# Block 0's W_O by seven products, the next operands from W_B on, and one scores matmul for two pairs

## The chip, the cores and the metric

The kernel runs on one core of a Trainium2 chip. The metric is the device time of one execution in microseconds, taken as the median of several runs. The profile names the engines PE (TensorE, matrix products), PEld (its weight loads), DVE (VectorE), ACT (ScalarE), POOL (GpSimd) and SP (SyncE, which here only issues DMA).

## The reference

One layer is computed for 2048 prompt tokens and 64 sample tokens, all in float32, model width 1024.

```
h = rms_norm(x, g_pre);  vA, bA, cA, zA, q, f, iv, zB, gA, gB = split(h @ w_in)     # ten 1024-wide parts
yA = (silu(zA) * bA * causal_conv3(cA * vA, conv_w)) @ w_a_out                      # path A
fg = lb + (1 - lb) * sigmoid(f);  k = 1 - fg;  qq = silu(q) * QK_SCALE              # path B, 8 heads of 128
per chunk of 64 tokens:
    att = tril(qe @ ke^T);  o = att @ v + (q * exp(b)) @ S;  S = exp(b_last) * S + (k * ...)^T @ v
yB = (rms(o) * g_onorm * silu(zB)) @ w_b_out
merged = sigmoid(gA) * yA + sigmoid(gB) * yB
x = x + rms_norm(merged @ w_o, g_post)
x = x + (p @ w_ple_proj) * sigmoid(rms_norm(x, g_ple) @ w_ple_gate)
```

The outputs are the new x of both streams and the end states of the convolution and of S.

## The kernel before

The 2112 tokens stand on the free axis, features on the 128 partitions. They are cut into three blocks of 704 columns, numbered 0, 1 and 2, and every block into two halves of 352 (`HN`). Each float32 operand is split into a rounded high part and the rest (`split`: a ScalarE copy and a VectorE subtraction), and each product is three matmuls: high by high, high by low, low by high. The weights are split likewise. In block 0 the low halves are made on VectorE and stored to DRAM under a key in `lows`; later uses load them (`split_w`). The stores go to SP's queue in block 0 and to POOL's queue from block 1 on.

Most of the large products save an eighth of their matmuls by taking seven products of quarter matrices instead of eight (Strassen's scheme in Winograd's form). In `sgroup` the seven run side by side for one pair of weight blocks. In `in_turn` they run one after the other over four groups each: a product's seven operands are made in turn by VectorE and ScalarE (`operand_of`) while the product before it runs, so that the operands of the whole stage need not be held. Both need four sums S1 to S4 of weight quarters, which stand in DRAM under `sums`; `combined` makes them in block 0 for the parts of w_in, `prepare_sums` for W_A, W_B and W_O (`w_a_out`, `w_b_out`, `w_o`), four groups for each matrix.

A block goes through these stages: eight heads of path B (`head_prep`, then `head_attn` in steps) mixed with gate products; path A (`path_a`); W_A; W_B with the merge by the gates; W_O; then the first gates of the next block, into which the norm of this block (`final_norm`) is spread, and the gate product W_G with the end of the layer (`final_gate`). In block 0, W_A, W_B and W_O are plain: `gemms` runs eight output blocks of 2 halves x 8 feature blocks x 3 matmuls, that is 48. In blocks 1 and 2 all three go by `in_turn`. The sums of W_A and W_B are prepared during W_A and W_B of block 0 (`sums_ahead`, from `merge`), those of W_O during path A of block 1.

While W_O runs, the operands of the next block's gates are made (`operands`: two x tiles are loaded and scaled, then eight combinations of their halves are formed and split; four such quarters). In block 0 this goes with W_O's output blocks 1, 3, 5 and 7, in block 1 through hooks. Hooks are small steps queued in `hooks`; one is taken after each product or group, so that their instructions stand in the queues right there. In block 0 the squares for the norm are summed as W_O's outputs come (`final_out`); in block 1 they are summed in the first hooks of the next gates (`squares`).

In a head, a pair is two chunks of 64 tokens. A block has five pairs and a lone chunk; four pairs stand in part 0, the fifth in part 1, the lone chunk in part 2. `head_prep` makes kb (a pair's keys, the first chunk scaled to the second) and ka (the first chunks' keys, unscaled). `head_attn` transposes kb and v on TensorE (L935, L937), then makes the scores: for each pair one matmul of ka by the first chunk's queries (L946, 64 columns) and one of kb by the second chunk's (L947). L946 takes 128 columns of ka, which hold the first chunks of two neighbouring pairs, and only one pair's half of the result is used. The mask `caus` and `copy_predicated` (L950, L951) put the scores into `att`. `sink_v` writes v by `into` (L412), one VectorE instruction for each half.

The order of the instructions on each engine is that of the program, moved by a scheduler that weighs priorities (`tc.high_priority`) and marks (`placed`, `behind_all`). Large tiles come from a ring of 52; PSUM has five banks for products (`pg`) and three for the rest (`pa`).

Of the kernel before, what the change touches and what calls it, by code (L numbers as in the profile page):

```python
# [90 lines left out]
def hybrid_step(  # L91
# [61 lines left out]
    caus = const.tile([P, P], I32, tag="caus", name="caus")  # L153
# [14 lines left out]
    def constants():  # L168
        tri = rt(P)
        G.memset(tri, 1.0)  # L170
        G.affine_select(
            out=tri, in_=tri, pattern=[[1, P]], compare_op=ALU.is_ge, fill=0.0, base=0, channel_multiplier=-1
        )
        V.tensor_copy(caus, tri)
# [414 lines left out]
    def gemms(idx0, act, segs, by_k=False, late=KB - 1):  # L589

        j0, j1 = 0, KB
        if len(segs) > 1:
            yield from gemm_late([idx0, idx0 + 1], act, segs, late)
            j0 = 2
        if by_k:
            j1 -= 2
        for j in range(j0, j1):
            yield gemm(idx0 + j, act, segs)
        if by_k:
            yield from gemm_by_k([idx0 + j for j in range(j1, KB)], act, segs)  # L600
# [235 lines left out]

    def head_prep(bl, hc, hd, first, hs):
# [24 lines left out]
        ka, kb, qx, vt, z = hf(HN + 32), rt(), rt(), rt(), rt()  # L862

        def scaled(after):
# [8 lines left out]
            for g in bl["groups"]:  # L873
# [6 lines left out]
            V.tensor_tensor(chunks(kb)[:, 1:nch:2, :], chunks(sf)[:, 1:nch:2, :], chunks(lg)[:, 1:nch:2, :], ALU.mult)  # L880
            V.tensor_tensor(
                chunks(kb)[:, 0 : 2 * npair : 2, :],
                ka3[:, :npair, :],
                f2.unsqueeze(2).to_broadcast([P, npair, CH]),
                ALU.mult,
            )
# [6 lines left out]
        def sink_v(c, h, x, y):  # L893
            if c == 1:
                into(half(vt, h), x, y)
# [13 lines left out]
    def head_attn(ip, gs, d, hd):  # L909
# [21 lines left out]

        p_k, p_v = ps_attn(), ps_attn()
# [9 lines left out]
        with placed():  # L942
            for i, g in enumerate(gs):
                o = g["off"]
                if not single:
                    T.matmul(p_a[:, i * P : i * P + CH], d["ka"][:, o // 2 : o // 2 + P], qe[:, o : o + CH], start=True, stop=True)  # L946
                T.matmul(p_a[:, i * P + CH : i * P + P], cols(d["kb"], g), qe[:, o + ln - CH : o + ln], start=True, stop=True)  # L947
        pa3 = cols3(p_a, nt)
        if not single:
            V.copy_predicated(att[:CH, :nt], caus[:CH].unsqueeze(1).to_broadcast([CH, nt, P]), pa3[:CH])  # L950
        V.copy_predicated(att[CH:, :nt, CH:], caus[CH:, CH:].unsqueeze(1).to_broadcast([CH, nt, CH]), pa3[CH:, :, CH:])  # L951
# [138 lines left out]
    def merge(bl, a, kept, extra):  # L1090

        segs = bl["segs"]
        ob, m, mg, loaded = [], [], [], {}
# [19 lines left out]
        for j, pss in enumerate(gemms(W_B, ob, segs)):  # L1113
# [8 lines left out]
        return mg  # L1122
# [34 lines left out]
    def final_out(segs, mg, xo, acc):  # L1157

        for j, pss in enumerate(gemms(W_O, mg, segs, True)):
            xo.append(rt())  # L1160
            for s, ps in zip(segs, pss):
                A.copy(xo[j][:, cols_of(s)], ps)
            if j < KB - 2:
                sum_squares(j, xo[j], acc, BN)
            yield
        for j in range(KB - 2, KB):
            sum_squares(j, xo[j], acc, BN)
        yield

# [20 lines left out]
    def final_norm(bl, segs, xo, acc, h2, kept, squares=False):  # L1190
# [15 lines left out]
        if squares:  # L1206
# [172 lines left out]
    for bi, bl in enumerate(blocks):  # L1379
# [10 lines left out]
        sums_ahead = prepare_sums((W_A, W_B), True) if first else prepare_sums((W_O,), False) if bi == 1 else iter(())  # L1390
# [17 lines left out]
        if first:  # L1408
            mg = merge(bl, a, kept, sums_ahead)
        else:  # L1410
            stages, loads = merge_in_turn(a, kept, mg)
            stages.append(out_in_turn(mg, xo, acc, bl["last"]))
            loads(W_A, -1)
            for idx, n in in_turn(stages, a_first):
                loads(idx, n)
                if nxt and (idx, n) == (W_B, 6):
                    hc = new_operands()
                    ops = operands(hc, spread_all(cols), partial(load_x, nxt), True)
                    spread_out((ops, (0, 1, 0, 1, 0, 1, 0) * KH))
                elif nxt:  # L1420
                    pass
                elif (idx, n) == (W_B, 5):
                    ph = [split_rt(raw) for raw in load_p(bl, G)]
                elif (idx, n) == (W_O, 4):
                    norms = [final_norm(bl, [s], xo, acc, h2, None) for s in segs]
                    spread_out((norms[0], (1, 0, 1, 1, 1, 0, 1, 0)))
            if nxt:
                xo.extend(stages[-1]["mid"])
        if nxt:
            if first:  # L1430
# [68 lines left out]
```

## Time and profile before

| | us |
|---|---|
| median of 3 runs | 2639.74 |
| lowest and highest | 2634.62, 2641.88 |
| the profiled execution | 2640.08 |
| its span | 2638.4 |
| TensorE busy in it | 2610.8 |
| VectorE, ScalarE, GpSimd busy | 1708.9, 1483.9, 360.0 |

The stages by the trace, in microseconds from the span's start: heads and path A of block 0 to 664.9, its W_A to 726.5, W_B to 788.2, W_O from 789.5 to 853.9, the first gates of block 1 to 956.5, W_G of block 0 to 1018.4. Block 1 has W_A from 1534.4, W_B from 1588.8, W_O from 1644.5 to 1702.1, then the gates of block 2 to 1807.4. A group's line in the profile reads: source line, engine, operation, written and read tiles, shape, count, then busy microseconds, mean nanoseconds of one, and the idle time before them with what ended it. A busy span of a matmul is longer than the step from one to the next, since they are pipelined; steps are read from start to start.

### The profile page before, as it was taken

The numbers are of one execution on the slowest core, as the hardware profiler recorded it, in microseconds if no ns is written. First come the engines' busy times: TensorE is split into PE (matmuls) and PEld (weight loads), VectorE is DVE, ScalarE is ACT, GpSimd is POOL, SyncE is SP. The second block draws the span as 40 slices with busy tenths as digits, with TensorE's granted clock in tenths as the row PEclk, the third lists the DMA queues.
The fourth block names the chain that finished last, engine by engine and source line by source line (L and its number), as shares of the span: only waits on it lengthen the run. The fifth ranks groups of instructions, "written<-read, shape, count | busy, mean of one in ns | idle before, by whom it ended". The sixth has DMA issues, their size and how long they took to land. (4 is left out here: it accounts for less than half of the span.)

```text
span 2638.4 us, 47798 instructions
## 1 busy us (share of the span) xinstructions
PE 2610.8 (99%) x16700; PEld 2593.0 (98%) x16700; DVE 1708.9 (65%) x3325; ACT 1483.9 (56%) x2892; POOL 360.0 (14%) x665
## 2 busy tenths in 40 slices
PE   8999999999999999999999999999999999999999
PEld 8999999999999999999999999999999999999998
DVE  7788888888666554665645569763356464337867
ACT  6666665554335644665645555664466564445664
POOL 1000000200432211111112211021000000001011
PEclk9999999999999999999999999999999999999999
DMA  8677777998998998767789989898767768888975
GB/s 308 225 269 274 246 279 263 313 312 283 377 339 288 346 307 276 222 198 265 224 286 360 378 309 329 282 357 310 255 222 226 232 221 263 272 271 311 310 243 186
DMA packets 364530, 741.29 MB, mean 281 GB/s; under 512 B 44448, under 2 KB 49088, under 8 KB 364288
## 3 DMA queue, kind: packets, MB, share of 16 engines
q1 hardware_dynamic: 326016, 590.30, 66.5%
q0 software_dynamic: 37984, 147.90, 15.4%
q8 instruction: 131, 2.15, 0.3%
q14 instruction: 111, 0.91, 0.1%
q10 hardware_dynamic: 288, 0.05, 0.0%
HBM read 532.00 MB, written 206.06 MB: 280 GB/s over the span
## 5 line engine op out<-in xcount | busy, mean ns | idle before, releaser
L366 PE MATMUL pg<-r,hi 128*128 128x352 f32 x3304 | 1095.3, 332 | 1.9 <-ACT hi L222 0.7
L367 PE MATMUL pg<-r,hi 128*128 128x352 f32 x3304 | 1068.0, 323 | 0.0
L368 PE MATMUL pg<-r,lo 128*128 128x352 f32 x2356 | 763.2, 324 | 2.8 <-DMA lo<-low 2.8
L222 ACT CAST hi<-raw 128x512 fp32r<-128x512 f32 x720 | 443.0, 620 | 569.8 <-PE pg L367 204.9
L366 PEld LDWEIGHTS pg<-r,hi 128*128 128x128 f32 x3304 | 622.8, 189 | 5.9 <-issue 3.7
L367 PEld LDWEIGHTS pg<-r,hi 128*128 128x128 f32 x3304 | 623.1, 189 | 0.0
L368 PEld LDWEIGHTS pg<-r,lo 128*128 128x128 f32 x2356 | 444.0, 188 | 3.5 <-DMA lo<-low 3.5
L368 PE MATMUL pg<-r,s 128*128 128x352 f32 x948 | 306.7, 323 | 0.8 <-DMA s<-low 0.8
L546 PE MATMUL pg<-r,hi 128*128 128x352 f32 x768 | 248.0, 324 | 0.5 <-ACT hi L192 0.5
L547 PE MATMUL pg<-r,hi 128*128 128x352 f32 x768 | 247.9, 323 | 0.3 <-DVE r L192 0.3
L192 ACT CAST hi<-raw 128x512 fp32r<-128x512 f32 x234 | 142.6, 619 | 160.3 <-PE pg L367 44.5
L548 PE MATMUL pg<-r,lo 128*128 128x352 f32 x688 | 222.5, 323 | 0.3 <-DVE lo L192 0.2
L512 PE MATMUL pg<-r,hi 128*128 128x352 f32 x656 | 212.4, 325 | 0.0
L511 PE MATMUL pg<-r,hi 128*128 128x352 f32 x656 | 209.4, 325 | 0.3 <-ACT r L192 0.2
L192 DVE TENSOR_TENSOR r<-r,r 128x352 fp32r<-128x352 f32 (+3 forms) x282 | 173.2, 633 | 54.6 <-ACT r L192 53.6
L192 DVE TENSOR_TENSOR lo<-raw,hi 128x512 fp32r<-128x512 f32 x234 | 159.2, 686 | 68.3 <-ACT hi L192 55.3
L192 ACT CAST r<-r 128x352 fp32r<-128x352 f32 (+3 forms) x282 | 153.2, 576 | 50.1 <-DVE r L692 15.1
L368 PEld LDWEIGHTS pg<-r,s 128*128 128x128 f32 x948 | 178.3, 188 | 1.2 <-DMA s<-low 1.1
L192 ACT CAST hi<-s 128x512 fp32r<-128x512 f32 x160 | 99.1, 619 | 141.9 <-PE pg L367 115.5
L380 ACT COPY hf<-pg 128x352 f32<-128x352 f32 x354 | 155.6, 447 | 5.1 <-PE pg L368 4.5
L546 PEld LDWEIGHTS pg<-r,hi 128*128 128x128 f32 x768 | 144.2, 188 | 1.2 <-ACT hi L192 0.8
L547 PEld LDWEIGHTS pg<-r,hi 128*128 128x128 f32 x768 | 144.3, 188 | 0.7 <-DVE r L192 0.6
(388 smaller groups left out, 4177.5 us busy)
## 6 DMA issues: line engine op xcount, KB each, us to landing
raw<-w_blk SPq DMA_DIRECT2D x586, 256.0 KB, 4.1
lo<-low SPq DMA_DIRECT2D x412, 256.0 KB, 4.0
raw<-S SPq DMA_DIRECT2D x408, 256.0 KB, 4.2
low<-lo SPq DMA_DIRECT2D x338, 256.0 KB, 3.8
s<-low SPq DMA_DIRECT2D x308, 256.0 KB, 3.9
S<-s SPq DMA_DIRECT2D x152, 256.0 KB, 3.3
r<-w_blk POOLq DMA_DIRECT2D x48, 256.0 KB, 7.3
S<-r POOLq DMA_DIRECT2D x48, 256.0 KB, 6.1
```

Of the source, the lines that this page charges most:

```text
L192: return A.copy(hi, src).ins, V.tensor_tensor(lo, src, hi.bitcast(F32), ALU.subtract).ins
L222: A.copy(hi, raw)
L366: add(hi[:, k, :], xhi, start=start and k == 0, stop=False)
L367: add(hi[:, k, :], xlo, start=False, stop=False)
L368: last[0] = add(lo[:, k, :], xhi, start=False, stop=k == KH - 1).ins
L380: copied = A.copy(got[n], ps[bank])
L511: add(hi[:, k, :], xhi, start=start and k == 0, stop=False)
L512: add(hi[:, k, :], xlo, start=False, stop=False)
L546: T.matmul(ps, hi[:, k % 4, :], xhi[:, c], start=k == ks[0], stop=False)
L547: T.matmul(ps, hi[:, k % 4, :], xlo[:, c], start=False, stop=False)
L548: last[0] = T.matmul(ps, lo[:, k % 4, :], xhi[:, c], start=False, stop=k == ks[-1]).ins
```

## The change

Block 0's W_O goes by `in_turn`, as in the other blocks, with `merge` handing over unsplit merged tiles. Its weight quarters have no stored low halves yet, so they are split and stored there. The sums of W_O and W_A are prepared in W_A and W_B of block 0, those of W_B in path A of block 1. The operands of the next block start earlier: one quarter in W_B (block 0 after output blocks 3, 5, 6 and 7, block 1 in hooks of products 5 and 6), the rest in hooks of W_O. The spread of the row norms by TensorE moves with them. The squares and the norm of block 0 follow the plan that block 1 has.

In the heads, the odd pairs hold their second chunk first. So one matmul of ka by the first chunks' queries of two pairs puts each pair's scores on the rows where that pair has its first chunk, and L946 becomes three matmuls a head instead of five, two of them 128 columns wide. For this kb is made by four instructions instead of two, v is written in eight pieces instead of two (`in_order`), and there is a second mask, so that the copies of part 0 go by even and odd pairs.

```
+        for rows, odd, base in ((slice(0, P), 0, 0), (slice(0, CH), 1, -CH), (slice(CH, P), 1, CH)):
...
-    def operands(hc, rs, load, early=False):
-        pair = None
+    def operands(hc, rs, load):
+        pair = [load(k) for k in (0, KH)]
+        yield
         for i in range(KH):
-            pair = pair or [load(k) for k in (i, i + KH)]
...
-            pair = [load(k) for k in (i + 1, i + 1 + KH)] if early and i + 1 < KH else None
+            pair = [load(k) for k in (i + 1, i + 1 + KH)] if i + 1 < KH else None
+    def in_order(nch, npair):
+        out = []
+        for c in range(nch):
+            g, second = divmod(c, 2)
+            to = CH * (c + (1 - 2 * second if g % 2 and g < npair else 0))
+            cut = HN if c * CH < HN < (c + 1) * CH else (c + 1) * CH
+            for lo, hi in ((c * CH, cut), (cut, (c + 1) * CH)):
...
+            for odd in range(2):
+                seconds = slice(1 + 2 * odd, 2 * npair, 4)
+                gs = slice(odd, npair, 2)
...
+                V.tensor_tensor(chunks(kb)[:, place[1], :], chunks(sf)[:, seconds, :], chunks(lg)[:, seconds, :], ALU.mult)
+                V.tensor_tensor(chunks(kb)[:, place[0], :], ka3[:, gs, :], scale, ALU.mult)
-                into(half(vt, h), x, y)
+                for o, end, to in pieces:
+                    if h * HN <= o < (h + 1) * HN:
+                        s = slice(o - h * HN, end - h * HN)
+                        V.tensor_tensor(vt[:, to : to + end - o], x[:, s], y[:, s], ALU.add)
-                if not single:
-                    T.matmul(p_a[:, i * P : i * P + CH], d["ka"][:, o // 2 : o // 2 + P], qe[:, o : o + CH], start=True, stop=True)
+                if not single and i % 2 == 0:
+                    both = slice(i, min(i + 2, nt))
+                    own = cols3(p_a, nt)[:, both, :CH]
+                    firsts = qe[:, o : o + (both.stop - i) * P].rearrange("p (g c) -> p g c", c=P)[:, :, :CH]
+                    T.matmul(own, d["ka"][:, o // 2 : o // 2 + P], firsts, start=True, stop=True)
-            mg.append(split_rt(sg))
+            mg.append(sg)
...
+            side(j)
-        sums_ahead = prepare_sums((W_A, W_B), True) if first else prepare_sums((W_O,), False) if bi == 1 else iter(())
+        sums_ahead = prepare_sums((W_O, W_A), True) if first else prepare_sums((W_B,), False) if bi == 1 else iter(())
+        stages = [out_in_turn(mg, xo, acc, bl["last"])]
+        if first:
+            def side_ops(j):
+                if j == KB - 2:
+                    a_first.extend(narrow(half(t, 0)) for t in mg[:KH])
+                if j in (3, 5, 6, 7):
+                    next_ops(1)
+            merge(bl, a, kept, mg, sums_ahead, side_ops)
...
+        rest = (0, 1, 0, 1, 0, 1, 0, 0, 0) * (KH - 1)
+        if first:
+            spread_out((ops, rest))
+        for idx, n in in_turn(stages, a_first):
+            loads(idx, n)
+            if nxt and (idx, n) == (W_B, 4):
+                next_ops(1)
+                spread_out((ops, (0, 0, 0, 1, 0, 1, 0, 1) + rest))
-                for j, _ in enumerate(final_out(segs, mg, xo, acc)):
-                    if j in (1, 3, 5, 7):
-                        run(ops, 3)
-            norm = final_norm(bl, segs, xo, acc, h2, kept, not first)
-            start = (0, 1, 0, 1) + (0, 1, 0) * KB if first else (1, 1, 1, 1, 0, 1, 0, 1) + (0, 1) * KB
+            norm = final_norm(bl, segs, xo, acc, h2, kept)
+            spread_out((norm, (1, 1, 1, 1, 0, 1, 0, 1) + (0, 1) * KB + (0, 1, 0, 1) + (0, 1) * KB))
```

More of the change, by code (lines that the diff above doesn't have):

```diff
@@ L587, in gemm_by_k, with gemms @@
         return pss
[L589 to L597, printed above, removed]
+    def gemms(idx0, act, segs):
+        yield from gemm_late([idx0, idx0 + 1], act, segs, KB - 1)
+        for j in range(2, KB):
             yield gemm(idx0 + j, act, segs)
-        if by_k:
-            yield from gemm_by_k([idx0 + j for j in range(j1, KB)], act, segs)
     def tiles_of(n):
@@ L1088, in reload, with merge @@
         return t
-    def merge(bl, a, kept, extra):
+    def merge(bl, a, kept, mg, extra, side):
         segs = bl["segs"]
-        ob, m, mg, loaded = [], [], [], {}
+        ob, m, loaded = [], [], {}
         def fetch(kind, j):
@@ L1205, in final_norm @@
             fetch()
-        if squares:
+        if kept is not None:
             for j in range(KB):
@@ L1407, in hybrid_step @@
         mg, xo, h2, acc = [], [], [], rt()
[L1408 to L1428, printed above, removed]
@@ new lines, in hybrid_step @@
+        if first:
[5 more added lines that the diff above has]
+            merge(bl, a, kept, mg, sums_ahead, side_ops)
+        else:
+            before, loads = merge_in_turn(a, kept, mg)
+            stages = before + stages
+            loads(W_A, -1)
+        rest = (0, 1, 0, 1, 0, 1, 0, 0, 0) * (KH - 1)
+        if first:
+            spread_out((ops, rest))
```

76 lines of the change are left out of this document (43 added, 33 removed).

## The prediction

> **What bounds the kernel now.** I read the page's head first, then a table of stages, then TensorE's waits, then single stretches of the timeline. The head:
>
> ```profile
> span 2638.4 us, 47798 instructions
> PE 2610.8 (99%) x16700; PEld 2593.0 (98%) x16700; DVE 1708.9 (65%) x3325; ACT 1483.9 (56%) x2892; POOL 360.0 (14%) x665
> ```
>
> TensorE is never idle for long, so time falls with every matmul that is taken out, as long as what feeds TensorE keeps up. The table gives, for each stretch, busy time and count by engine, then granted clock, share of the DMA engines and GB/s. In order the rows are: W_B of block 0, W_O of block 0, the gates of block 1, W_B of block 1, W_O of block 1, the gates of block 2, and two stretches used below.
>
> ```profile
> 726.50:788.20 61.70, 61.70 (x386) 61.70 (x385) 42.11 (x68) 21.29 (x35) 23.83 (x45) 1.00 0.95 341
> 789.50:853.90 64.40, 63.28 (x387) 61.91 (x386) 46.34 (x70) 31.59 (x59) 14.22 (x27) 1.00 0.82 286
> 853.90:956.50 102.60, 101.04 (x638) 99.97 (x637) 57.40 (x89) 65.31 (x120) 16.97 (x29) 1.00 0.94 336
> 1588.80:1643.20 54.40, 54.40 (x337) 53.98 (x336) 48.17 (x104) 32.05 (x68) 6.40 (x12) 1.00 0.95 327
> 1644.50:1702.10 57.60, 56.42 (x340) 53.97 (x339) 50.47 (x97) 40.54 (x84) 4.28 (x8) 1.00 0.86 290
> 1702.10:1807.40 105.30, 102.38 (x637) 101.51 (x637) 58.49 (x88) 66.62 (x120) 17.68 (x31) 0.98 0.95 339
> 1745.00:1760.00 15.00, 13.05 (x72) 12.76 (x71) 8.58 (x13) 9.77 (x18) 2.49 (x5) 0.89 1.04 400
> 90.00:105.00 15.00, 12.78 (x78) 12.17 (x77) 10.39 (x22) 6.73 (x13) 0.00 (x0) 0.89 0.67 226
> ```
>
> W_B of block 0 runs its 384 matmuls in 61.7 us: 0.161 us a matmul with nothing waiting. W_O of block 0 needs 64.4 for the same number, 2.7 lost. W_O of block 1 already goes by seven products: 336 matmuls would be 54.0 at that pace and take 57.6, with VectorE busy 50.47. What TensorE waited for in the whole run:
>
> ```profile
> PE pa L1062 <- ACT r L192: 6.9, 1, 6.9
> PE pg L368 <- DMA lo<-low: 2.8, 2, 1.9
> PE pa L937 <- DVE r L412: 1.8, 1, 1.8
> PE pg L368 <- DMA s<-low: 0.8, 1, 0.8
> PE pa L935 <- DVE r L881: 0.4, 1, 0.4
> ```
>
> The first is the start of the program and is not touched. The others are weights late from DMA in the gates, and the transposes of the first head.
>
> **W_O of block 0.** Eight plain blocks of 48 matmuls become seven products of four groups of 12: 48 matmuls fewer, 7.7 us at 0.161. What replaces them is VectorE and DMA work on a stage in which both are loaded; the nearest row is W_O of block 1. Two things differ there. In block 0 the low halves of W_O's own quarters are not yet in DRAM, so 12 blocks are split on VectorE; and a quarter of the next block's operands has been made in W_B before. Their prices:
>
> ```profile
> L192 DVE TENSOR_TENSOR lo<-raw,hi 128x512 fp32r<-128x512 f32 x234 | 159.2, 686 | 68.3 <-ACT hi L192 55.3 <-DMA raw<-w_blk 6.1 <-DMA low<-lo 4.6
> L705 DVE SCALAR_TENSOR_TENSOR r<-r,vec,r 128x704 f32<-128x704 f32 x24 | 22.3, 946 | 3.5 <-DMA r<-x_fm 3.5
> L192 DVE TENSOR_TENSOR r<-r,r 128x704 fp32r<-128x704 f32 x82 | 72.4, 888 | 36.5 <-ACT r L192 36.1
> L192 DVE TENSOR_TENSOR r<-r,r 128x352 fp32r<-128x352 f32 x176 | 87.6, 519 | 18.0 <-ACT r L192 17.4
> ```
>
> And SP's loads of weights, KB each and us to landing:
>
> ```profile
> raw<-w_blk SPq DMA_DIRECT2D x586, 256.0 KB, 4.1
> ```
>
> The splits add 12 x 0.686 = 8.2. A quarter of the operands is two scalings, five half-width instructions and three full-width splits: 2 x 0.946 + 5 x 0.519 + 3 x 0.888 = 7.2. So VectorE has 50.5 + 8.2 - 7.2 = 51.5 to do in a stage that could last 54.0, which gives 57.6 + 1.0 = 58.6 by block 1's losses. The DMA side is worse than in block 1. SP now issues 28 blocks, 16 loads of lows and 12 stores of 256 KB, 24 more than the 16 loads and 16 stores of before: 6.3 MB on top of the 18.4 that 286 GB/s moved in 64.4 us, less one pair of x tiles: near 24 MB, 400 GB/s over 60 us, which is the rate of the stretch 1745 to 1760, where a late low held TensorE. On SP a block's load stands behind the store of a block some five earlier, which waits for VectorE's split; at 1.9 us a block that is about 10 us ahead, so one late split does not stop TensorE but several in a row do. I add 1.4 for this: 60.0, a gain of 4.4. Ends: 54.0 with no loss (gain 10.4), and 65.8, where W_O of block 1 pays for all splits and the moved quarter comes late (a loss of 1.4). The value lies nearer the slow half because both resources are filled.
>
> W_B of block 0 takes over a quarter of the operands (7.2) and half-width splits of four merged tiles (2.1) and gives up full-width splits of all eight (8 x 0.888 = 7.1): 44 busy of 61.7, so nothing there; its POOL queue gets four x loads behind the stores of the sums, and the loads of gB queue behind these, a stage ahead of need. If that cover is gone, W_B waits for gB; bound 0 to +2, taken as 0. The 8 groups of sums are the same number as before, W_O's first, and W_B's now stand where W_O's stood in block 1: 0. The six-matmul spread between W_B and W_O moves into W_B: 0.
>
> **W_O of block 1.** A quarter of the operands leaves it for the end of W_B, where VectorE has 54.4 - 48.17 = 6.2 us free against 7.2. So about 1 us falls back into W_O, whose VectorE load drops to 44. It can win at most its 3.6 lost; I take 1.5, with ends of -3.6 and +1.5 (the backlog meets the first products).
>
> **The gates of block 1.** The sums of squares of W_O's result move from W_O into the first hooks of these gates, which gives them the plan that the gates of block 2 have. These need 105.3 against 102.6, two of the DMA waits above among them. I take half the difference, +1.4; ends -2 (its own waits vanish) and +2.7.
>
> **The scores matmuls.** In a head, four pairs stand in one part, one pair and the lone chunk in others. The first-half product (L946) goes from five matmuls to three a head. Each is two records:
>
> ```profile
> L946 PE MATMUL pa<-r,hf x240: 217/275/294, 97.4 to 2165.1; 128*128 128x64 f32 x120
> 1154.40 0.60 PE L937 MATMUL pa<-ident,r 128*128 128x128 f32 x4
> 1154.84 0.33 PE L946 MATMUL pa<-r,hf 128*128 128x64 f32 x2
> ...
> 1156.54 0.41 PE L366 MATMUL pg<-r,hi 128*128 128x352 f32 x1
> 156.99 1.05 PE L957 MATMUL pa<-r,r 128*128 128x128 f32 x8
> 157.80 0.41 PE L366 MATMUL pg<-r,hi 128*128 128x352 f32 x1
> ```
>
> From 1154.84 to 1156.54 sixteen 64-wide records take 1.70 us, 0.106 each; eight 128-wide ones take 0.81, 0.101 each. So twice the columns cost no more, and each of the 48 matmuls removed (two a head, 24 heads) is worth its full 2 x 0.106 to 0.112: 10.2 to 10.7 us; I take 10.4. The other end is 0, if the two runs of columns with a gap between them cost twice; no row shows such an operand.
>
> **VectorE in the heads.** The second chunk of every odd pair now stands first, so v is written in 8 pieces instead of 2, kb by 4 instructions instead of 2, and the mask by 4 instead of 2. The last v piece must be there when TensorE reaches L937:
>
> ```profile
> 1149.39 0.19 DVE L888 COPY r<-hf 128x64 f32<-128x64 f32 x1
> 1149.61 0.52 DVE L386 TENSOR_TENSOR hf<-hf,pg 128x352 f32<-128x352 f32 x1
> 1150.05 0.16 DVE L889 TENSOR_TENSOR qc<-qc 128x5 f32<-128x5 f32 x1
> 1150.12 0.74 DVE L1013 SCALAR_TENSOR_TENSOR r<-pa,vec,r 128x512 f32<-128x512 f32 x1
> 1151.85 0.51 DVE L412 TENSOR_TENSOR r<-hf,hf 128x352 f32<-128x352 f32 x1
> 1152.28 0.51 DVE L412 TENSOR_TENSOR r<-hf,pg 128x352 f32<-128x352 f32 x1
> 1152.71 0.51 DVE L901 TENSOR_TENSOR r<-pg,r 128x352 f32<-128x352 f32 x1
> ```
>
> v is ready at 1152.79 and needed at 1154.40: 1.6 us of slack. A start costs 0.43 at 352 columns and 0.07 at five, so some 0.07 an instruction; eight more give 0.6, and the z product (L901) now stands ahead of the second half: 0.43. The chain grows by about 1.0, and 0.6 of slack is left. With the 0.22 that the 64-wide copy takes, 0.15 an instruction, it grows by 1.6 and just fits. In block 0 VectorE is busier, and one or two heads may wait: +0.5, ends 0 and +5. The mask's two extra pieces end long before the product that reads it. The first head, already late (1.8 and 0.4 above), gets the longer chain and one more 0.686 split ahead of its last piece: +1.2, ends 0.4 and 2.
>
> [...]
>
> **The sum**, against the profiled execution's 2640.1 (span 2638.4; the median is 2639.7): -4.4 - 1.5 + 1.4 - 10.4 + 0.5 + 1.2 = -13.2, so 2627. All good ends together give -26, 2614.
>
> **Rivals.** First, W_O of block 0 becomes bound by VectorE and the weights' path, and keeps nothing: 65.8, 5.8 more than taken, 2633. For it: 51.5 of 54.0 and 400 GB/s. Against it: W_O of block 1 lives with 50.5 and loses 3.6 only. A stall can cost more than its length, since in 1745 to 1760 a 1.9 us wait left a mean clock of 0.89, another 1.7 us, as the first head's 2.2 us did in 90 to 105; one such in W_O is in this rival. [...]
>
> Second, on the other side, the heads wait for v. Its place is L937 in all 24 heads; its price is whatever the chain grows beyond 1.6 us. It makes the change a loss by over 0.3% from about 0.9 us a head (13 + 8 over 24), that is with a chain 2.5 us longer, or 0.26 us for each of the eight extra instructions. At 1.0 a head the time is 2651. For it: block 0's VectorE also carries weight splits that can slip in between the pieces. Against it: the 0.07 above.
>
> Third, the merged scores matmul is not cheaper than the two it replaces: 2637. Against it: the eight 128-wide records in 0.81 us.
>
> **How the numbers follow.** The forecast has 0.68, the first rival 0.16, the second 0.10, the third 0.06. 0.3% is 7.9 us and about what a measurement of this kernel can tell, so the border is 2631.8. The forecast lies below it but for a small part, the first rival around it with a third below, the third inside: faster 0.72, same 0.17, slower 0.11. The range runs from the good ends, 2614, to the third rival, 2638, and leaves out the second and a little at the bottom.
>
> **What would show it.** Right: 96 fewer scores records and about 0.44 us less a head from one head to the next; W_O of block 0 in 57 to 62 us with VectorE over 85% busy; W_O of block 1 in 55 to 57; gates of block 1 near 104; TensorE's waits still single. Wrong: L937 waiting on the v pieces in most heads; W_O of block 0 over 64, with waits on lows or on VectorE's operands; a granted clock under 1.00 in it; merged records spaced over 0.2 us.

## The result

The changed kernel takes **2651.52 us** (median of 6 runs, 2646.97 to 2653.13), the kernel before 2639.05 (6 runs, 2634.62 to 2641.88): a ratio of 1.0042 with a 95% interval of 1.0029 to 1.0056. It is slower by about 12 us, where the prediction had 2627, a range of 2614 to 2638, and 0.72 for faster. The profiled execution of the changed kernel took 2652.05 against 2640.08.

The head of its page:

```profile
span 2650.3 us, 47894 instructions
PE 2599.9 (98%) x16556; PEld 2577.1 (97%) x16556; DVE 1744.6 (66%) x3619; ACT 1494.7 (56%) x2924; POOL 362.2 (14%) x669
```

TensorE has 144 records fewer, as the change says (48 matmuls of 352 columns and 96 scores records), and is busy 10.9 us less. The span is 11.9 us longer all the same, so TensorE is idle some 23 us more. The table by stages, with the columns as before; the rows are W_A of block 0, W_B, W_O, the gates of block 1, and W_O of block 1:

```profile
673.60:735.40 61.80, 61.80 (x386) 61.80 (x385) 44.39 (x70) 24.06 (x39) 28.02 (x52) 1.00 0.99 373
735.40:809.70 74.30, 68.00 (x398) 67.01 (x397) 51.66 (x88) 24.09 (x43) 31.67 (x59) 0.93 0.95 347
809.70:870.00 60.30, 56.12 (x338) 53.86 (x337) 54.45 (x105) 39.90 (x82) 7.00 (x13) 1.00 0.95 333
870.00:975.00 105.00, 103.02 (x638) 101.58 (x637) 58.74 (x88) 65.87 (x119) 17.90 (x31) 0.98 0.94 335
1660.30:1719.70 59.40, 56.53 (x340) 54.41 (x339) 53.53 (x106) 41.81 (x85) 4.29 (x8) 1.00 0.84 290
```

W_O of block 0 has 48 matmuls fewer and takes 60.3 where it took 64.4. But W_B of block 0, which runs the same matmuls as before, takes 74.3 where it took 63.0 (from 726.5 to 789.5, the start of W_O). What TensorE waited for, the rows that are new (line, releaser, us in total, times, longest):

```profile
PE pg L367 <- DVE r L911: 7.0, 7, 1.0
PE pg L367 <- DVE hf L406: 5.2, 7, 0.7
...
PE pg L547 <- ACT hi L193: 3.2, 1, 3.2
PE pg L549 <- DVE lo L193: 3.1, 1, 3.1
```

The first two are in the heads, seven times each, so once a head after the first one of block 0: a product (L367) waits for a PSUM bank that VectorE still reads, once for the pieces of v (L911), once for an addition behind them (L406). The last two are the two long waits of W_B. So the loss has two places. How far one head lies from the next is read from the first transposes of kb (L935 before, L952 after). Two heads of block 0 and two of block 1, before and after:

```profile
147.41 0.38 PE L935 MATMUL pa<-ident,r 128*128 128x128 f32 x2
196.52 0.38 PE L935 MATMUL pa<-ident,r 128*128 128x128 f32 x2
1047.39 0.38 PE L935 MATMUL pa<-ident,r 128*128 128x128 f32 x2
1082.88 0.49 PE L935 MATMUL pa<-ident,r 128*128 128x128 f32 x3
```

```profile
148.05 0.38 PE L952 MATMUL pa<-ident,r 128*128 128x128 f32 x2
198.59 0.38 PE L952 MATMUL pa<-ident,r 128*128 128x128 f32 x2
1065.92 0.38 PE L952 MATMUL pa<-ident,r 128*128 128x128 f32 x2
1100.97 0.49 PE L952 MATMUL pa<-ident,r 128*128 128x128 f32 x3
```

In block 1 a head comes 35.05 us after the one before it instead of 35.49: 0.44 less, what two merged scores matmuls are worth. In block 0 it comes 50.54 after instead of 49.11: 1.4 more, so about 1.9 us a head are lost there, counted from a head that had won the 0.44.

The stages of all runs, each from its first 352-wide matmul to that of the next stage, from the profiled executions (us), with the median and the ratio to the kernel before of the same chip (95% interval). E1 to E10 are the experiments below. The columns `heads` hold the eight heads and path A behind them; path A is 224 to 227 us of it, in every block and run but two:

| | heads 0 | W_B 0 | W_O 0 | gates 1 | heads 1 | W_O 1 | heads 2 | median | ratio |
|---|---|---|---|---|---|---|---|---|---|
| before | 586.2 | 63.0 | 64.4 | 102.6 | 516.0 | 57.6 | 514.3 | 2639.1 | |
| after | 592.6 | 74.3 | 60.4 | 104.9 | 513.4 | 59.1 | 510.3 | 2651.5 | 1.0042 (1.0029 to 1.0056) |
| E1 | 582.8 | 75.1 | 57.8 | 103.6 | 516.1 | 59.0 | 514.5 | 2646.5 | 1.0036 (1.0025 to 1.0047) |
| E2 | 592.6 | 63.0 | 62.0 | 103.2 | 512.2 | 57.4 | 510.1 | 2637.4 | 1.0003 (0.9993 to 1.0013) |
| E3 | 594.4 | 67.4 | 69.5 | 103.9 | 513.6 | 59.1 | 510.4 | 2655.8 | 1.0067 (1.0052 to 1.0082) |
| E4 | 581.5 | 75.3 | 58.2 | 102.3 | 512.4 | 59.0 | 510.3 | 2633.7 | 0.9987 (0.9977 to 0.9996) |
| E5 | 594.4 | 64.3 | 54.2 | 102.8 | 525.2 | 59.0 | 510.3 | 2648.6 | 1.0039 (1.0025 to 1.0053) |
| E6 | 593.9 | 73.7 | 60.3 | 106.7 | 513.3 | 59.1 | 509.7 | 2656.6 | 1.0068 (1.0052 to 1.0084) |
| E7 | 582.0 | 67.2 | 54.2 | 102.8 | 525.7 | 59.0 | 511.4 | 2635.2 | 0.9985 (0.9975 to 0.9994) |
| E8 | 580.5 | 65.4 | 54.2 | 102.9 | 517.6 | 58.9 | 509.9 | 2625.7 | 0.9951 (0.9934 to 0.9968) |
| E9 | 581.4 | 63.8 | 63.4 | 102.5 | 511.1 | 57.6 | 510.1 | 2626.9 | 0.9952 (0.9938 to 0.9965) |
| E10 | 577.7 | 64.0 | 54.2 | 104.3 | 522.8 | 59.0 | 510.4 | 2631.4 | 0.9970 (0.9957 to 0.9983) |

Two columns are left out that move without an edit. The time up to the first head's products lies between 78.1 and 82.9 us in the twelve profiles (78.7 before, 81.0 after; 82.2 in E4, whose profiled execution, 2640.1, is the slowest of that kernel's runs). The gates of block 2 lie between 103.0 and 107.5. In E5 and E7 path A of block 1 takes 238.0 and 238.3 us. Differences of a stage of 1 or 2 us that show in one run alone are not read as effects.

### The profile page after: what moved, and what is told of

It reads as the page before. It is cut to its first block, busy times and chain, and to the rows that moved or that the text cites. A ratio compares the mean times of both kernels' runs of the same rounds, so it can differ in the third digit from the quotient of the medians.

```text
span 2650.3 us, 47894 instructions
## 1 busy us (share of the span) xinstructions
PE 2599.9 (98%) x16556; PEld 2577.1 (97%) x16556; DVE 1744.6 (66%) x3619; ACT 1494.7 (56%) x2924; POOL 362.2 (14%) x669
## 3 DMA queue, kind: packets, MB, share of 16 engines
q1 hardware_dynamic: 329472, 596.59, 67.2%
## 5 line engine op out<-in xcount | busy, mean ns | idle before, releaser
L367 PE MATMUL pg<-r,hi 128*128 128x352 f32 x3304 | 1094.5, 331 | 13.7 <-DVE r L911 7.0
L223 ACT CAST hi<-raw 128x512 fp32r<-128x512 f32 x736 | 453.0, 620 | 571.3 <-PE pg L368 217.1
L369 PE MATMUL pg<-r,lo 128*128 128x352 f32 x2356 | 760.7, 323 | 1.3 <-DMA lo<-low 1.3
L367 PEld LDWEIGHTS pg<-r,hi 128*128 128x128 f32 x3304 | 622.6, 188 | 19.2 <-ACT hi L193 15.9
L368 PEld LDWEIGHTS pg<-r,hi 128*128 128x128 f32 x3304 | 622.4, 188 | 0.0
L193 ACT CAST hi<-raw 128x512 fp32r<-128x512 f32 x230 | 140.9, 620 | 181.3 <-PE pg L368 65.1
L512 PE MATMUL pg<-r,hi 128*128 128x352 f32 x752 | 239.7, 325 | 2.4 <-ACT r L193 2.0
L547 PE MATMUL pg<-r,hi 128*128 128x352 f32 x640 | 208.6, 327 | 3.2 <-ACT hi L193 3.2
L193 DVE TENSOR_TENSOR r<-r,r 128x352 fp32r<-128x352 f32 (+3 forms) x298 | 178.5, 618 | 48.8 <-ACT r L193 48.3
L193 DVE TENSOR_TENSOR lo<-raw,hi 128x512 fp32r<-128x512 f32 x230 | 157.0, 688 | 59.1 <-ACT hi L193 53.4
L549 PE MATMUL pg<-r,lo 128*128 128x352 f32 x556 | 181.6, 327 | 3.1 <-DVE lo L193 3.1
L193 ACT CAST hi<-s 128x512 fp32r<-128x512 f32 x160 | 99.2, 620 | 140.5 <-PE pg L368 116.1
L193 ACT CAST r<-r 128x352 fp32r<-128x352 f32 (+3 forms) x298 | 157.5, 563 | 27.3 <-DVE r L686 10.1
L514 PE MATMUL pg<-r,lo 128*128 128x352 f32 x508 | 164.6, 324 | 2.6 <-DMA lo<-low 2.6
L513 PEld LDWEIGHTS pg<-r,hi 128*128 128x128 f32 x752 | 141.5, 188 | 5.1 <-DVE r L193 4.4
```

What stands on the lines that cost most here:

```text
L193: return A.copy(hi, src).ins, V.tensor_tensor(lo, src, hi.bitcast(F32), ALU.subtract).ins
L223: A.copy(hi, raw)
L367: add(hi[:, k, :], xhi, start=start and k == 0, stop=False)
L368: add(hi[:, k, :], xlo, start=False, stop=False)
L369: last[0] = add(lo[:, k, :], xhi, start=False, stop=k == KH - 1).ins
L512: add(hi[:, k, :], xhi, start=start and k == 0, stop=False)
```

## The two parts by themselves (E1, E2)

The theory after the result: there are two losses with two causes, the heads of block 0 and W_B of block 0. The rival: it is one cause, a backlog of VectorE that comes out of block 0's heads and is carried on. Two runs take the change apart.

**E1, the changed kernel with the heads of before**: `constants`, `head_prep` and the scores part of `head_attn` are those of before, and `in_order` is gone.

```diff
-                for o, end, to in pieces:
-                    if h * HN <= o < (h + 1) * HN:
-                        ...
+                into(half(vt, h), x, y)
...
-                if not single and i % 2 == 0:
-                    ...
+                if not single:
+                    T.matmul(p_a[:, i * P : i * P + CH], d["ka"][:, o // 2 : o // 2 + P], qe[:, o : o + CH], start=True, stop=True)
```

> The changed kernel with the heads of before (v in two pieces, kb in two, one mask, five first-half scores products a head): only the part from W_B of block 0 on is changed. Theory, the loss has two separate places: the first head of each pair of block 0 goes back from 50.6 to 49.1 us and the heads of blocks 1 and 2 from 35.1 to 35.5; W_A and W_B of block 0 still need about 136 us (124.6 in before), since two groups of sums still stand on VectorE ahead of the first merge of W_B; W_O of block 0 about 60. Time 2646 to 2651. Rival, VectorE's backlog comes out of the heads and is carried into W_B: W_A and W_B fall to 125 or 126 us and the time is 2635 to 2638.

Measured: 2646.5. The heads of block 0 are back at 49.1 us apart (582.8 in all), and W_B still takes 75.1. The rival's 2635 to 2638 is out: what W_B loses does not come from the heads.

**E2, the kernel before with the merged scores alone**:

```diff
-    caus = const.tile([P, P], I32, tag="caus", name="caus")
+    caus = [const.tile([P, P], I32, tag=f"caus{i}", name=f"caus{i}") for i in range(2)]
...
+    def in_order(nch, npair):
...
-                into(half(vt, h), x, y)
+                for o, end, to in pieces:
...
-                if not single:
+                if not single and i % 2 == 0:
```

> The kernel before with nothing but the merged scores products (and the order of v, kb and mask that they need). Theory: heads of block 0 50.6 us apart, those of blocks 1 and 2 35.1; W_A and W_B of block 0 124.6 as in before, because the sums stand behind the second merge; all else as in before. The gain of 16 x 0.45 = 7 in blocks 1 and 2 and the loss of 7 x 1.5 in block 0 leave 2639 to 2643. Rival, the heads of block 0 are slow for another part of the change: 49.1 - 0.45 us apart, 2628 to 2630.

Measured: 2637.4, a ratio of 1.0003, a little under the 2639 to 2643 of the theory. The heads of block 0 lose 6.4 us, those of blocks 1 and 2 win 3.8 and 4.2, and W_B is at 63.0 as before. So the two parts lose separately: the part from W_B on about 9 us of the 12, the scores nothing on balance, since what they win in two blocks they give away in the third.

## Where the heads of block 0 lose (E4)

VectorE before TensorE's first wait in one head of block 0. First the kernel before (start, us, line, tile):

```profile
185.50 0.69 DVE L300 TENSOR_TENSOR s<-raw,raw 128x512 f32<-128x512 f32 x1
186.10 0.52 DVE L412 TENSOR_TENSOR r<-hf,pg 128x352 f32<-128x352 f32 x1
186.53 0.52 DVE L391 TENSOR_TENSOR hf<-hf,hf 128x352 f32<-128x352 f32 x1
```

Then the changed one, and TensorE's matmul that waits:

```profile
185.82 0.69 DVE L301 TENSOR_TENSOR s<-raw,raw 128x512 f32<-128x512 f32 x1
186.42 0.55 DVE L911 TENSOR_TENSOR r<-hf,pg 128x128 f32<-128x128 f32 x3
186.88 0.69 DVE L193 TENSOR_TENSOR lo<-raw,hi 128x512 fp32r<-128x512 f32 x1
187.48 0.25 DVE L911 TENSOR_TENSOR r<-hf,pg 128x96 f32<-128x96 f32 x1
...
187.88 0.40 PE L367 MATMUL pg<-r,hi 128*128 128x352 f32 x1 [0.97 <-DVE r L911]
```

In the kernel before one instruction reads the PSUM bank (`pg`) and is done by 186.62; in the changed one the bank is free only when the fourth piece is done, and a weight split of 0.69 us stands between the third and the fourth. TensorE stands still for 0.97. E4 asks whether it is this order or the amount of work.

```diff
                         s = slice(o - h * HN, end - h * HN)
-                        V.tensor_tensor(vt[:, to : to + end - o], x[:, s], y[:, s], ALU.add)
+                        with tc.high_priority():
+                            V.tensor_tensor(vt[:, to : to + end - o], x[:, s], y[:, s], ALU.add)
```

> The changed kernel with the eight v pieces of a head at high priority, so that VectorE makes them ahead of the weight splits; nothing else is changed. Theory A, the order is at fault (a split or a sum of 0.69 us stands between the pieces while TensorE waits for the bank that they read): the wait of 1.0 us a head at the first half's pieces falls under 0.3 and the heads of block 0 come 49.5 us apart or less, 2641 to 2644. Theory B, VectorE has too much to do in that stretch of a head, whatever the order: another wait takes its place, the heads stay at 50.4 to 50.8 and the time at 2649 to 2653.

Measured: 2633.7, a ratio of 0.9987 (0.9977 to 0.9996): below the kernel before, and 8 us better than theory A had it. The heads of block 0 come 48.4 to 50.0 us apart and take 581.5 in all, 11 less than in the changed kernel, and the two rows of waits at L367 are gone. The same stretch of that run (the time axis is that of E4):

```profile
181.39 0.88 DVE L904 TENSOR_TENSOR r<-r,qc 128x704 f32<-128x704 f32 x1
182.19 0.71 DVE L912 TENSOR_TENSOR r<-hf,pg 128x128 f32<-128x128 f32 x4
182.82 0.69 DVE L301 TENSOR_TENSOR s<-raw,raw 128x512 f32<-128x512 f32 x1
```

The four pieces stand together, ahead of the sums and splits, and hold VectorE for 0.63 us from the first start to the next instruction. VectorE has the same work as in the changed kernel; the order was at fault. W_B stays at 75.3 here too.

## Where W_B of block 0 loses (E3, E5, E6)

VectorE in the changed kernel's W_B. L341, L343, L345 and L347 make the four sums of one group from blocks that POOL has loaded (`r<-w_blk`), L341 first; L193 with `lo<-raw,hi` is the split of W_B's own weights, for which TensorE waits:

```profile
738.42 0.52 DVE L1135 TENSOR_TENSOR r<-pg,r 128x352 f32<-128x352 f32 x1
742.89 0.69 DVE L341 TENSOR_TENSOR r<-r,r 128x512 f32<-128x512 f32 x1 [3.95 <-issue]
...
744.95 0.68 DVE L193 TENSOR_TENSOR lo<-raw,hi 128x512 fp32r<-128x512 f32 x1
...
757.84 0.69 DVE L341 TENSOR_TENSOR r<-r,r 128x512 f32<-128x512 f32 x1 [3.72 <-DMA r<-w_blk]
```

POOL's queue shows when those blocks were asked for:

```profile
733.61 1.07 POOL L324 DMA_DIRECT2D r<-w_blk  x2
737.04 1.08 POOL L324 DMA_DIRECT2D r<-w_blk  x2 [2.36 <-issue]
```

The last load of the group is issued by 738.1 and the sums begin at 742.89; in this stage such a load took 5.7 us to land (the median of four, 733 to 744). VectorE stands still before it for 3.95 us; the profile names no releaser there (`issue`), but does name the load at 757.84, the second time. The split at 744.95 that TensorE needs stands behind. TensorE waits 3.06 us at 745.69 and, with the second group, 3.24 at 761.04, there for a high half from ScalarE (L547 above). In the kernel before the sums of the same place in the program stand after the first two merges, 15 us after their loads; the scheduler now puts two groups ahead of the first merge, and why it does so is not known. A VectorE that stands still for such a load is not a loss in itself: in W_A of both kernels it does so twice for 3.1 to 3.7 us, and W_A loses nothing (61.7 and 61.8). E3 restores the order of before by hand.

**E3, the sums held behind the merge before:**

```diff
-            V.tensor_tensor(sg, sg, m[j], ALU.add)
+            added.append(V.tensor_tensor(sg, sg, m[j], ALU.add).ins)
             mg.append(sg)
             if j in (0, 2, 4, 6, 7):
-                next(extra, None)
+                with behind_all(added[j - 1 : j]):
+                    next(extra, None)
```

> The changed kernel, where each group of sums that is made in W_B of block 0 is held behind the sum of the merge before, as VectorE's order has it in the kernel before; nothing else is changed. Theory, VectorE stands still in its order for the loads of these groups and TensorE waits for the splits behind them: W_A and W_B of block 0 fall from 136 to 125 or 126 us, with no wait over 1 us in W_B, and the time to about 2641. Rival, VectorE or DMA has too much to do in W_B (51.7 us busy in 74, a quarter of the operands and its four loads added): the waits move, W_A and W_B stay over 132, 2648 or more.

Measured: 2655.8, slower still. W_B falls to 67.4, but W_O rises to 69.5; together they take 136.9 where the changed kernel has 134.7. The two stages of that run:

```profile
735.50:802.90 67.40, 65.17 (x397) 64.58 (x397) 45.82 (x78) 21.80 (x38) 28.90 (x54) 0.97 1.01 374
802.90:872.50 69.60, 59.85 (x339) 57.80 (x338) 60.70 (x114) 43.07 (x88) 9.66 (x18) 0.88 0.88 298
```

VectorE is busy 60.7 us in W_O, whose 336 matmuls need 54.2, and ScalarE's and VectorE's splits of the operands come late (`L512 <- ACT r L193`, 8.1 us in two waits, and 1.7 for a split by VectorE); the granted clock is 0.88 over the stage. So the order of the sums explains where the wait shows, not that there is one: neither theory as it was written holds. In the kernel before three groups of sums ran in W_B at no cost, and the fourth ran into W_O (800.3 to 804.3), where plain blocks left VectorE idle (46.3 of 64.4 busy). That W_O by seven products has no such room, so that the sums have to be over by its start, is what E5 puts to the test.

**E5, W_A's sums made elsewhere**, so that W_B of block 0 has no more of them than the end of W_O's. By the edit and the trace the new place is path A of block 1, ahead of W_B's sums (the eight groups stand from 1308 to 1505, path A from 1305 to 1543); the expectations of E5, E7 and E8 call it the last heads of block 1:

```diff
-        sums_ahead = prepare_sums((W_O, W_A), True) if first else prepare_sums((W_B,), False) if bi == 1 else iter(())
+        sums_ahead = prepare_sums((W_O,), True) if first else prepare_sums((W_A, W_B), False) if bi == 1 else iter(())
...
-                if j >= 3:
+                for _ in range(2 if j == 0 else 1):
                     next(sums_, None)
```

> The changed kernel, where the sums of W_A are made in the last heads of block 1, ahead of those of W_B, and no longer in W_B of block 0 (W_O's four groups alone stay in block 0, and they are over by the start of W_B); the heads' pieces are as in the changed kernel. Theory, the four groups of sums with their loads, casts and stores are what holds the queues of VectorE, ScalarE and POOL in W_B: W_A and W_B of block 0 need 124 to 126 us, W_O of block 0 keeps 58 to 61, the heads of block 1 stay at 513 to 516, time 2638 to 2642. Rival, the quarter of the next block's operands with its loads of x is at fault: W_B stays over 70 us, 2649 or more. Third, the sums cost the same in their new place: heads of block 1 over 520.

Measured: 2648.6. The rows are W_B and W_O of block 0, and the heads of block 1 with path A:

```profile
734.70:799.00 64.30, 63.42 (x398) 63.13 (x397) 40.83 (x71) 16.78 (x29) 9.60 (x18) 1.00 0.72 253
799.00:853.20 54.20, 54.20 (x339) 53.99 (x338) 47.38 (x88) 39.19 (x80) 3.21 (x6) 1.00 0.94 320
1017.80:1543.00 525.20, 515.05 (x3349) 509.25 (x3349) 311.99 (x746) 308.41 (x594) 108.69 (x213) 1.00 0.86 297
```

W_B is at 64.3, and W_O of block 0 runs at 54.2 without a wait: its full gain of 10.2 us. The DMA engines' share of W_B falls from 0.95 to 0.72, and W_B and W_O move 33.6 MB (253 x 64.3 + 320 x 54.2) instead of 45.9, 12.3 MB less: the loads and stores of the four groups. But the heads of block 1 with path A take 11.8 us more than in the changed kernel, all of it in path A (238.0 against 226.2), where TensorE now waits 7.0 us for VectorE and 2.8 for DMA. The theory's stages and the third case are both right, the theory's time (2638 to 2642) is not: the sums are the cause in W_B, and they cost as much in their new place. They do not cost that much everywhere: the four groups that path A of block 1 held already cost about 2 us there at most (226.2 against 224.3 in block 2, which makes none).

**E6, the operands begun later** (with the last merge of W_B, the quarter then made in W_O):

```diff
-                if j in (3, 5, 6, 7):
+                if j == 7:
                     next_ops(1)
...
-            spread_out((ops, rest))
+            spread_out((ops, (0, 1, 0, 1, 0, 1, 0) * KH))
```

> The changed kernel, where the next block's operands are begun with the last merge of W_B of block 0 instead of after the fourth, so that the quarter is made in W_O; the sums stay. Theory, the sums hold W_B: it stays at 73 to 76 us, and W_O of block 0 takes the quarter's 7.2 us of VectorE and comes to 60 to 64; 2651 to 2656. Rival, the quarter of the operands holds it: W_B falls to 63 to 65, 2641 to 2644.

Measured: 2656.6, with W_B at 73.7 and W_O at 60.3. The other load that was put on W_B, the quarter of the operands, is not what holds it. It seems to have a price in W_O: the last sums are made by 795.6, before W_O starts at 808.6, and W_O, which now makes the quarter, still takes 60.3 where E5 has 54.2.

## Putting both right (E7 to E10)

**E7** has E4's priority and E5's place of the sums together:

```diff
+                        with tc.high_priority():
...
+        sums_ahead = prepare_sums((W_O,), True) if first else prepare_sums((W_A, W_B), False) if bi == 1 else iter(())
```

> Both cures together: the v pieces at high priority, and the sums of W_A made in the last heads of block 1. If the two losses are separate, the gains add: heads of block 0 about 581 us, W_A and W_B of block 0 124 to 126, W_O of block 0 58 to 60, time 2619 to 2625, below the kernel before by 13 to 18. Rival, VectorE in block 0 has only so much room, and what is gained in W_B comes back as waits in W_O or in the gates of block 1: 2627 to 2634.

Measured: 2635.2. The gains in block 0 add (heads 582.0, W_O 54.2), but block 1 pays as in E5 (525.7, of which path A 238.3), so that nothing is left beside E4's 2633.7. The expectation had left out that price, which the third case of E5, written at the same time, had named. In E4 the DMA share was 0.93 to 1.04 from 1340 to 1500, in path A, and about 0.7 in the first four heads; E8 goes there.

**E8, one group a head in the first four heads of block 1:**

```diff
             hooks.append(partial(keep_z, hd, d["z"]))
+            next(extra, None)
...
-        path_b(bl, hc, first, kept, fills, hs if first else None)
+        path_b(bl, hc, first, kept, fills, hs if first else None, prepare_sums((W_A,), False) if bi == 1 else iter(()))
...
-        sums_ahead = prepare_sums((W_O, W_A), True) if first else prepare_sums((W_B,), False) if bi == 1 else iter(())
+        sums_ahead = prepare_sums((W_O,), True) if first else prepare_sums((W_B,), False) if bi == 1 else iter(())
```

> The changed kernel with the v pieces at high priority, and with the sums of W_A made one group a head in the first four heads of block 1, where the DMA share was 0.69 to 0.71 and VectorE busy 22 of 35 us in the run with the pieces first; in the last 200 us of those heads, where the run before this put them, the share was 0.93 to 1.04. Theory, the sums cost TensorE time only where the DMA engines are full: W_B of block 0 stays at 64 to 68 us and W_O of block 0 at 54, as without them, and the heads of block 1 at 512 to 515 instead of 525.7; time 2620 to 2626. Rival, the sums hold VectorE's order wherever they stand (each group's four loads, casts and stores in one queue): heads of block 1 at 520 or more, 2630 to 2636.

Measured: 2625.7, a ratio of 0.9951 (0.9934 to 0.9968). The rows are again W_B, W_O and the heads of block 1 with path A:

```profile
722.70:788.00 65.30, 63.72 (x397) 63.07 (x397) 42.50 (x74) 17.76 (x31) 10.17 (x19) 1.00 0.74 259
788.00:842.20 54.20, 54.20 (x338) 53.99 (x337) 47.38 (x88) 39.20 (x80) 3.22 (x6) 1.00 0.94 320
1006.90:1524.50 517.60, 513.48 (x3351) 509.63 (x3350) 311.00 (x746) 309.15 (x594) 109.41 (x213) 1.00 0.87 302
```

The sums still cost 5.2 us in the heads of block 1 (517.6 against 512.4 in E4), less than half of E7's 13.3: three of them come 36.4, 37.2 and 50.9 us after the one before instead of 35.1, 35.1 and 49.5 in E4 (the last with a part between that is no head). The time is the theory's, the 517.6 lies between theory and rival. That the free DMA engines make the difference is not shown: path A also holds four other groups of sums.

**E9, the kernel before with the merged scores and the pieces first**, without any other part of the change; the edit is E2's and E4's together:

```diff
-                into(half(vt, h), x, y)
+                for o, end, to in pieces:
...
+                        with tc.high_priority():
+                            V.tensor_tensor(vt[:, to : to + end - o], x[:, s], y[:, s], ALU.add)
```

> The kernel before with the merged scores products alone, and the v pieces at high priority; W_O of block 0, W_B and the sums are those of before. Theory, what the scores are worth by themselves: heads of block 0 580 to 582 us, of block 1 512, of block 2 510, all else as in before (W_B 63, W_O 62 to 64.4): 2626 to 2630. The distance to the run with the sums in the heads (2625.7) is then what W_O by seven products is worth after its costs, by the stage tables 1 to 3 us. Rival, the pieces' order takes from VectorE's other work in block 0 what it gives: 2634 or more.

Measured: 2626.9, a ratio of 0.9952 (0.9938 to 0.9965): not to be told from E8. The part of the change from W_B on wins 7.6 us in W_B and W_O (119.6 against 127.2) in E8, and pays 6.5 in the heads of block 1 with path A and 1.3 in W_O of block 1. After its costs it is worth about nothing. All the gain of the better version is in the heads. At 0.44 a head the merged scores make 10.6 of it; in block 0 the gain is 4.8 where eight heads would give 3.5, so some of it may be the priority's own. The kernel before with the priority alone was not run.

**E10, two sums a head over eight heads** instead of four over four:

```diff
             keep("S3", i1, a21)
+            if halves:
+                yield
...
+            for _ in range(2 if hd == 0 else 1):
+                next(extra, None)
```

> As the run with the sums of W_A in the heads of block 1, but two sums a head over eight heads instead of four sums a head over four. Theory, VectorE's stretch of a group (four sums, four splits, 5.5 us in a row) delays the masks and the states of the head it falls in; two at a time fit: the first heads of block 1 come 35.1 to 35.6 us apart instead of 36.4 and 37.2, the heads of block 1 together 513 to 515, time 2621 to 2624. Rival, each sum costs the same wherever it stands: heads of block 1 517 to 518, 2625 to 2627.

Measured: 2631.4. Its interval overlaps E8's, but the heads of block 1 with path A take 522.8 against 517.6: three heads lose 1.4, 3.8 and 4.7 us. In the second of them VectorE stands still for a load of the sums again, with a mask (L979) behind it that TensorE needs:

```profile
1151.54 0.69 DVE L341 TENSOR_TENSOR r<-r,r 128x512 f32<-128x512 f32 x1 [3.54 <-DMA r<-w_blk]
1152.26 0.69 DVE L343 TENSOR_TENSOR r<-r,r 128x512 f32<-128x512 f32 x1
1152.99 0.69 DVE L347 TENSOR_TENSOR r<-r,r 128x512 f32<-128x512 f32 x1
1153.71 0.23 DVE L979 COPY_PREDICATED att<-caus,pa 64x64 f32<-64x64 int32 x1
1153.97 0.69 DVE L349 TENSOR_TENSOR r<-r,r 128x512 f32<-128x512 f32 x1
```

The edit did not do what it was meant to. L341, L343, L347 and L349 are the four sums of one group, and they still stand together in one head; only the groups have moved apart. So neither theory was put to the test. What the two runs do show is that a group whose load had landed cost nothing: VectorE did not wait for the first one (L341 at 1036.63 in E8, 1036.44 in E10), and that head took 35.1 and 35.2 us; for the other three of each run it waited 2.4 to 4.5 us, and each cost 1.4 to 4.7. The two dear ones of E10 are a wait of TensorE and a lower clock together: it waited 2.24 and 2.88 us, and the granted clock was 0.75 from 1154.5 to 1161.3 and 0.76 from 1243.2 to 1250.2, which is 1.7 us more each time.

## Why the prediction was wrong

**W_O of block 0, -4.4: right.** It measured -4.0. The number is in part luck. The waits are of the kinds that were named (2.6 us for low halves from DMA, 1.6 for splits by VectorE), but the limit was not this stage's own work (E5 and E8: 54.2, VectorE 47.4 busy, 17.3 MB); it was the sums that run into it from W_B, which had no term there. Its DMA traffic was put at 24 MB and is 20.1 with the sums (333 x 60.3). The first rival (65.8) falls.

**W_B of block 0, taken as 0 with an end of +2: wrong, +11.3.** This is the step that failed most. The prediction named the POOL queue and the loads of gB as the cover that could go. What came late were the loads of the sums, which it had set at 0 because their number is the same. It did not ask where they had room before: three groups behind merges of W_B at no cost, and the last group in W_O's idle VectorE time, which the same change took away. E5 shows the size: without the four groups W_B takes 64.3. Two waits of 3.1 and 3.2 us and a granted clock of 0.93 over 74.3 us (an estimate of 5.2 from the table's row) make up the 11.3. That a stall costs more than its length stood in the first rival, but for W_O and not for W_B.

**The scores, -10.4: right for two blocks.** Blocks 1 and 2 won 2.6 and 4.0 in all, 0.44 a head, as counted. The third rival falls.

**The heads, +0.5 with an end of +5: wrong, about 10 in block 0.** Its heads took 6.4 more, though the merged scores are worth 3.5 there too. The price of a piece was right: four pieces hold VectorE 0.63 us where one whole instruction holds it 0.43, 0.07 for each extra one. Wrong was the place: v was followed to the transposes that read it (slack 1.6 us, which it kept: L954 waits once, 0.6), and not to the PSUM bank that the additions free for the next product, where block 0 had no slack: about 1 us a head at L911 and 0.7 behind it, and E4 takes both away by the order alone. The condition that splits slip in between the pieces stood in the second rival and decided it.

**The second rival** had the time (2651) and a part of the cause (VectorE's pieces in the heads), but all 24 heads at L937; it was seven heads of block 0 at another line, and half of the loss was elsewhere.

**The first head, +1.2:** it lost nothing; its wait at the transposes of v went from 1.8 to 0.6.

**W_O of block 1, -1.5: wrong, +1.5**, the bad end. All runs with this part of the change have 58.9 to 59.1, those without 57.4 to 57.6. VectorE is busy 53.5 of 59.4 there, and the waits are for splits of operands; which of the moved pieces does it was not tried.

**The gates of block 1, +1.4:** +2.3, but by luck: 1.7 of it is a granted clock of 0.51 from 927.4 to 930.8, behind a wait of 1.1 us. Four runs with the same plan (E4, E5, E7 and E8) have 102.3 to 102.9, as the 102.6 of before.

## What to carry to other kernels

A wait has a second end: an instruction that is cut into pieces holds its source until the last of them is done, here a PSUM bank, for which TensorE's product waited 0.97 us behind the fourth piece, so look for the next writer of what it reads and not only for the reader of what it writes. When a stage gets shorter, ask what the other stages had been leaving in it: background work with its loads and stores (12.3 MB here) does not vanish, and in the heads it cost nothing where its loads had landed before its turn in VectorE's order, and 1.4 to 4.7 us a group where they had not. Look in the trace whether an edit moved what it was meant to move: in E10 it did not. Take a change of two parts apart before judging it: here one line of priority made the scores, worth nothing in E2, worth some 11 us in E9, and the part from W_B on was worth about nothing in the best place found for its sums.

## What the runs showed of the hardware that was not expected

A wait of 3.06 us was followed by a lower clock, as were those of 1.78 us at 97.12 and 1.95 us at 1747.35 in the kernel before (0.73 and 0.57 over the 4 us behind them). The matmuls behind it, in W_B of the changed kernel:

```profile
745.69 0.43 PE L549 MATMUL pg<-r,lo 128*128 128x352 f32 x1 [3.06 <-DVE lo L193]
...
746.72 0.49 PE L548 MATMUL pg<-r,hi 128*128 128x352 f32 x1
747.02 0.49 PE L549 MATMUL pg<-r,lo 128*128 128x352 f32 x1
...
749.66 0.42 PE L549 MATMUL pg<-r,lo 128*128 128x352 f32 x1
749.91 0.32 PE L547 MATMUL pg<-r,hi 128*128 128x352 f32 x1
```

They come 0.294 us apart from 746.72 to 749.66 instead of 0.161, ten of them, some 1.3 us on top of the wait; the granted clock is 0.51 from 746.4 to 749.9, and 0.51 again from 760.1 to 767.0, at the second wait. The length of the wait alone does not settle it: in the changed kernel a wait of 1.10 us (926.25) stands ahead of the 0.51 in the gates of block 1, and behind one of 1.76 us (846.13) the granted clock was 1.00 to 858; in E5 TensorE waited 3.10 us at 1317.41, and the granted clock was 1.00 from 1310 to 1328.

A scores matmul whose moving operand and whose output both skip every second 64 columns cost no more here than one without gaps: the heads of blocks 1 and 2 became shorter by the full 0.44 us for two matmuls less, and in the changed kernel the twelve scores records of a head's four pairs take 1.26 us (1066.79 to 1068.05) where sixteen took 1.70, 0.105 each as before.
